# A decoder block on one core: the networks' down products and the mixers' output held by tokens, with the weights as the 512-wide moving operand

## The chip, the core and the metric

The kernel runs on one core of one Trainium2 chip. The metric is the device time of one execution in microseconds. The engines are TensorE (PE, with its weight loads PEld), VectorE (DVE), ScalarE (ACT), GpSimd (POOL) and SyncE (SP); each works through its own instructions in order, and they wait for each other by semaphores.

## What is computed

A decoder block on 512 tokens of 1024 features, all in fp32:

```python
h = x
h = h + 0.5 * swiglu(rms_norm(h, g_ffn1), w_gate1, w_up1, w_down1)      # hidden width 2816
z = rms_norm(h, g_mix) @ w_in                                          # conv GLU | q | k | v | gates
y_conv = conformer_conv(a_glu, ...)                                    # depthwise, width 31
y_attn = (dilated window attention, 3 groups of 4 heads) @ w_attn_out
h = h + (sigmoid(gA) * y_conv + sigmoid(gB) * y_attn) @ w_mix_out
h = h + 0.5 * swiglu(rms_norm(h, g_ffn2), w_gate2, w_up2, w_down2)
h = h + sigmoid(rms_norm(h, g_ple) @ w_ple_gate) * (p @ w_ple_proj)
y = rms_norm(h, g_final)

def swiglu(x, w_gate, w_up, w_down):
    return (silu(x @ w_gate) * (x @ w_up)) @ w_down
def rms_norm(x, g):
    return x * rsqrt(mean(x * x, -1) + EPS) * g
```

## The kernel before

A product of two fp32 matrices is made of three matmuls on rounded operands: each operand is split into a high and a low part (`xsh`, `xsl`; `wh`, `wl`; `bh`, `bl`), and high x high, high x low and low x high are summed in PSUM (`mm3`, L458 to L460). A split is a copy by ACT that rounds and a subtraction by DVE. For most weights the low part is made by a copy of the negated high part and a DMA from POOL's queue that adds the raw weights (L374, L376).

The activations are held by features: a tile of 128 features by 512 tokens. The weights are the stationary operand and the tokens move. The tokens stand in four classes of 128 (token modulo four), since the attention needs them so; `by_class` reads a tile in that order, with a stride of four elements, and `classes` writes or reads one that is already in it. In before the order is made at the first network's last adds (L723) and in the first convolution products.

Each network's gate and up products run over eleven pairs of 128 hidden features. Two pairs (`EARLY = 2`) are plain products, 512 wide; the nine others are done in quarters, seven products in place of eight (`quarters_of`, L712, L713, L715), each 256 columns wide, with sums of weight quarters (L342 to L355) and of operand halves (`normed`, L806 for x; `form_pair`, L643, by POOL for the hidden values). The plain pairs need only the scaled x, since the norm's factor per token, R, is multiplied into their results (L774, L777). R comes from `Norm`: ACT squares (L567), DVE adds the squares (L575), PE sums them over the features (`ss`, L586), DVE finds the root by tokens (`by_token`, L589 to L594), writes it on diagonals (L598), and PE spreads it over all partitions (`on_all`, L603, L604). Then `normed` makes x times gain times R (`xn`, L811) and forms the nine pairs' operands from it.

Down products are made in three rounds of three pairs (`ROUNDS`), each for two groups of four feature tiles, in quarters, 256 tokens wide; then one plain round (`down_plain`). `add` (L727, L730) adds them to the residual `h`, times one half. The same quarters make the mixers' output (`mx`). At the end of a network, `into` splits the new residual for the next step, tile by tile. The last step, the gate of the per-layer embedding, works by tokens, and turns `h` there with transposes (`turned`, L1615).

The order of the work is the order in which the code issues it: `PLAN` lists the steps of a network, `slab` fetches, sums and splits weights some steps ahead, and jobs put aside (`job`) are issued by `work(t)` for as long as they fit into t us of ACT and DVE, or one by one after products (`QUOTA`, `AFTER`). `N_NORM` says in which plain pair, half and k the norm's two steps are issued. `background` issues the rotary tables' rows (`TABLES`, `TABLES_D`).

## Time and profile before

| | us |
|---|---|
| median of 3 runs | 1283.06 (1282.82 to 1283.29) |
| the profiled execution's span | 1280.8 |
| first network | about 0 to 354 |
| projections, convolution, attention, gates | about 354 to 829 |
| mixers' output | about 829 to 870 |
| second network | about 870 to 1210 |
| embedding gate and last norm | about 1210 to 1281 |

The span runs from the first to the last instruction of one profiled execution. Rows of a timeline give start, busy time, engine, line of the code, operation and tile, shape and count, and in brackets how long the engine was idle ahead of it and what ended that. Rows of the groups give count, busy time in all and mean ns of one, then the idle time ahead of them. Rows of the windows give from and to, the length, and for PE, PEld, DVE, ACT and POOL the busy time and the count of instructions, then the granted clock, the busy share of the DMA engines and GB/s. PE's matmuls overlap, so that their rows are longer than the distance between them.

### The profile page before, as it was taken

To read this page: it belongs to the slowest core of one execution; us is meant where nothing else is said; L and a number is where in the kernel's file an instruction comes from. 1 tells how busy PE (TensorE), PEld (TensorE's weight loads), DVE (VectorE), ACT (ScalarE), POOL (GpSimd) and SP (SyncE) were. 2 spreads that over 40 slices of the span, in tenths; PEclk is the share of its full clock that TensorE was granted. 3 is DMA by queue.
4 is the path that set the end of the run, shared out by engine and by line. 5 is a ranking of instruction groups with operands and counts; after the bars stand their busy time and mean duration, and the time that the engine had idled before them with its cause. 6 is when DMAs were issued, how large, how long until landed. Compare 5 with 4: busy or idle time off the path is not lost.

```text
span 1280.8 us, 21791 instructions
## 1 busy us (share of the span) xinstructions
PE 1267.4 (99%) x8266; PEld 1163.6 (91%) x8266; DVE 1015.3 (79%) x1617; ACT 740.9 (58%) x1088; POOL 299.8 (23%) x392
## 2 busy tenths in 40 slices
PE   9999999999999999999999999999999999999997
PEld 7899999998988888989898888898899999998986
DVE  6988778898969887878778755786988888786875
ACT  6677566575643264746565445373677566585662
POOL 3122222132223232333232222012122122132000
PEclk9999999999999999999999999999999999999999
DMA  9676876867879889898887788657576876867641
GB/s 302 148 171 161 204 201 157 206 165 191 193 177 227 213 152 204 155 188 150 173 183 166 168 190 218 160 119 211 132 177 159 203 206 146 208 168 187 155 115 50
DMA packets 114128, 226.12 MB, mean 177 GB/s; under 512 B 20584, under 2 KB 50664, under 8 KB 114024
## 3 DMA queue, kind: packets, MB, share of 16 engines
q0 software_dynamic: 49600, 142.10, 54.6%
q1 hardware_dynamic: 64136, 82.37, 20.1%
q8 instruction: 65, 1.06, 0.3%
q14 instruction: 39, 0.32, 0.1%
q10 hardware_dynamic: 288, 0.26, 0.1%
HBM read 168.56 MB, written 2.13 MB: 133 GB/s over the span
## 4 chain that ended last, share of the span: by engine, by line
PE 76%; DVE 2%; issue 0%; ACT 0%; DVEq 0%
PE pa L712 5%; PE pa L713 5%; PE pa L715 5%; PE pq L458 4%; PE pq L459 4%; PE pq L460 4%; PE pg L458 3%; PE pg L460 3%; PE pg L459 3%; PE pd L713 3%; PE pd L715 3%; PE pd L712 3%; PE pb L459 2%; PE pb L460 2%; PE pb L458 2%; PE pe L713 1%
## 5 line engine op out<-in xcount | busy, mean ns | idle before, releaser
L376 POOL DMA_DIRECT2D wl<-wr x108 | 93.4, 867 | 440.4 <-ACT wl L374 341.1
L712 PE MATMUL pa<-bh,wh 128*128 128x256 f32 x680 | 167.6, 284 | 0.5 <-DVE gx L727 0.4
L713 PE MATMUL pa<-bl,wh 128*128 128x256 f32 x680 | 167.3, 283 | 0.0
L1098 DVE SCALAR_TENSOR_TENSOR acc<-glu,taps,acc 128x511 f32<-128x511 f32 (+14 forms) x240 | 161.6, 732 | 0.0
L405 DVE TENSOR_TENSOR wl<-s,wh 128x1024 fp32r<-128x1024 f32 (+1 forms) x96 | 108.5, 1132 | 38.0 <-ACT wh L404 37.8
L374 ACT ACTIVATE wl<-wh 128x1024 fp32r<-128x1024 f32 x84 | 87.9, 1051 | 81.9 <-DMA wh<-in_w_in 50.8
L712 PEld LDWEIGHTS pa<-bh,wh 128*128 128x128 f32 x680 | 130.6, 192 | 1.0 <-issue 0.5
L713 PEld LDWEIGHTS pa<-bl,wh 128*128 128x128 f32 x680 | 130.8, 192 | 0.0
L374 ACT ACTIVATE wl<-wr 128x1024 fp32r<-128x1024 f32 (+1 forms) x108 | 105.7, 979 | 24.3 <-DVE wl L405 11.4
L404 ACT ACTIVATE wh<-s 128x1024 fp32r<-128x1024 f32 (+1 forms) x96 | 93.0, 969 | 38.8 <-PE pd L459 14.7
L388 ACT ACTIVATE wh<-wr 128x1024 fp32r<-128x1024 f32 (+1 forms) x108 | 105.5, 977 | 11.0 <-PE pd L715 6.1
L712 PE MATMUL pd<-bh,wh 128*128 128x256 f32 x448 | 110.3, 284 | 0.0
L713 PE MATMUL pd<-bl,wh 128*128 128x256 f32 x448 | 110.2, 283 | 0.0
L376 POOL DMA_DIRECT2D wl<-in_w_in x56 | 48.5, 869 | 219.6 <-ACT wl L374 200.5
L715 PE MATMUL pa<-bh,wl 128*128 128x256 f32 x680 | 97.0, 283 | 0.0
L458 PE MATMUL pq<-xsh,wh 128*128 128x512 f32 x224 | 88.8, 396 | 0.0
L715 PEld LDWEIGHTS pa<-bh,wl 128*128 128x128 f32 x680 | 88.4, 192 | 0.0
L459 PE MATMUL pq<-xsl,wh 128*128 128x512 f32 x224 | 87.4, 390 | 0.0
L460 PE MATMUL pq<-xsh,wl 128*128 128x512 f32 x224 | 87.4, 390 | 0.0
L713 PEld LDWEIGHTS pd<-bl,wh 128*128 128x128 f32 x448 | 86.2, 192 | 0.0
L712 PEld LDWEIGHTS pd<-bh,wh 128*128 128x128 f32 x448 | 86.1, 192 | 0.1
L458 PE MATMUL pg<-xsh,wh 128*128 128x512 f32 x192 | 76.1, 396 | 0.2 <-ACT xsh L478 0.2
(330 smaller groups left out, 3616.0 us busy)
## 6 DMA issues: line engine op xcount, KB each, us to landing
wl<-wr POOLq DMA_DIRECT2D x72, 512.0 KB, 5.7
wh<-in_w_in POOLq DMA_DIRECT2D x56, 512.0 KB, 7.0
wl<-in_w_in POOLq DMA_DIRECT2D x56, 512.0 KB, 6.0
wr<-in_w_ffn_up SPq DMA_DIRECT2D x80, 256.0 KB, 4.4
wr<-in_w_ffn_gate SPq DMA_DIRECT2D x78, 256.0 KB, 4.8
wr<-in_w_ffn_down SPq DMA_DIRECT2D x96, 192.0 KB, 3.8
wl<-wr POOLq DMA_DIRECT2D x36, 384.0 KB, 4.4
wr<-in_w_ffn_down SPq DMA_DIRECT2D x16, 256.0 KB, 4.1
```

The lines of the kernel that those rows point to most:

```text
L374: A.activation(l.bitcast(F32R), h, AF.Copy, scale=-1.0)
L376: G.dma_start(to, src, accum_op=OP.add)
L388: A.activation(h, r, AF.Copy)
L404: A.activation(h, r, AF.Copy)
L405: V.tensor_sub(l, r, h.bitcast(F32))
L458: PE.matmul(ps, wh, xh, start=start, stop=False, skip_group_check=part)
L459: PE.matmul(ps, wh, xl, start=False, stop=False, skip_group_check=part)
L460: PE.matmul(ps, wl, xh, start=False, stop=stop, skip_group_check=part)
L712: PE.matmul(o, h[:, c], th, start=q in ("B11", "B21", "T1") and i == 0, stop=False, skip_group_check=True)
L713: PE.matmul(o, h[:, c], tl, start=False, stop=False, skip_group_check=True)
L715: PE.matmul(o, l[:, c], th, start=False, stop=i >= len(at) - 2, skip_group_check=True)
L1098: bg.append(lambda acc=acc, g=g, w=w, s=s: V.scalar_tensor_tensor(acc[:, s:], g[:, :S - s], w, acc[:, s:], op0=OP.mult, op1=OP.add))
```

## The change

The residual `h` is now held by tokens: four blocks of 128 tokens by 1024 features. In the down products and the mixers' output the hidden values (or the mixed ones) are the stationary operand, and the weights move, 512 wide, read in four pieces of 128 (`rows_of`, L738 to L743). A round of down products takes two pairs and makes all features, so that there are five rounds; `EARLY` is 1, and ten gate and up pairs are done in quarters. The adds work on 512 features of a token block, with the factor per token `half_r` (0.5 r, L863), in which up's R is held.

```diff
-EARLY = 2
-ROUNDS = ((0, 2), (2, 3), (5, 3), (8, 3))
+EARLY = 1
+ROUNDS = ((0, 1), (1, 2), (3, 2), (5, 2), (7, 2), (9, 2))
-N_NORM = {"1": ((0, 1, 2), (0, 1, 7)), "2": ((0, 0, 6), (0, 1, 3))}
+N_NORM = {"1": ((1, 2), (1, 7)), "2": ((0, 6), (1, 3))}
+    def rows_of(ps, q, h_, l_, xs_, beside=None):
+        h_, l_ = (z.rearrange("p (m k i) -> p k m i", m=4, k=len(xs_)) for z in (h_, l_))
+        at = [(ps[g], slice(g * P, (g + 1) * P), k, *x_) for k, x_ in enumerate(xs_) for g in range(2)]
+        for o, c, k, th, tl in at:
+            PE.matmul(o, th[:, c], h_[:, k], start=q in ("B11", "B21", "T1") and k == 0, stop=False, skip_group_check=True)
+            PE.matmul(o, tl[:, c], h_[:, k], start=False, stop=False, skip_group_check=True)
+        if beside:
+            beside()
+        for o, c, k, th, tl in at:
+            PE.matmul(o, th[:, c], l_[:, k], start=False, stop=k == len(xs_) - 1, skip_group_check=True)
+    def add(q, ps, factor=None):
+        x_, half = GOES[q]
+        for i, p in enumerate(ps):
+            b = 2 * half + i
+            t = h[b][:, x_ * S:(x_ + 1) * S]
+            if factor is None:
+                V.tensor_add(t, t, p)
+            else:
+                V.scalar_tensor_tensor(t, p, factor[:, b:b + 1], t, op0=OP.mult, op1=OP.add)
```

The pairs' operands are formed from the scaled x without R: three of the quarters' operands are the plain pair's own splits, the sums come from `u`, a copy of the scaled x (in the first network by ACT at L1070, in the second beside each new split at L1086). R is multiplied into the gate's results (L918). The forming is issued between the two halves of the plain pair:

```diff
+            for c in range(4):
+                for q, (k, half) in {"B11": (c, lo), "B21": (c + 4, lo), "B22": (c + 4, hi)}.items():
+                    xn[c][q] = tuple(z[:, half] for z in xs[k])
+            u = made()
+        done = []
+        for half in range(2):
+            us_ = [slab(("gq", n, 0, 2 * half + i)) for i in range(2)]
+            fs = {k: f for (at, k), f in zip(N_NORM[n], (token, lambda: R.append(norm.on_all()))) if at == half}
+            if soon_ and half == 0:
+                fs[2] = soon_
+            done.append(plain(us_, fs))
+            if half == 0:
+                forms()
                 work(10.9)
-        xs.clear()
-        done = R = None
+        gated(*done)
+        work(10.9)
@@ gate_up
+                    if q != "T3":
+                        zs = z.rearrange("p (c s) -> p c s", s=256)
+                        r_ = both_halves(lo if q == "B21" else hi)
+                        job(lambda zs=zs, r_=r_: V.tensor_mul(zs, zs, r_), 0, 0.69)
@@ begin
-            xs.append(split(x[c], "xs", gain(V_G1, c)))
+            xs.append(split(by_class(x[c]), "xs", gain(V_G1, c), by=classes))
```

The classes' order is thus made at the very start, by strided reads. Where the layouts meet there are transposes by PE: of x into `h` during the first gate and up pair (`row_block`, L1077, 32, with strided stationary operands), and of `h` into the next step's operands at three places (`flipped`, L764, 96, four feature tiles between the two passes of the last product T4, four after the next step's k = 1). The 32 of the last step are gone. Where the norms are of `h`, the squares are summed by ACT while it squares (`Rows`, L624), without PE's `ss`. The pairs' subtractions are issued on DVE:

```diff
-    def form_pair(x1, x2, parts_, tile_=None, first_of=None, by=FORMS):
+    def form_pair(x1, x2, parts_, tile_=None, first_of=None, by=V):
+    class Rows(Norm):
+        def add(self, b, x_):
+            A.activation(T("sq"), h[b][:, x_ * S:(x_ + 1) * S], AF.Square, scale=D ** -0.5,
+                         accum_out=self.cols[:, x_ * NB + b:x_ * NB + b + 1])
+    def flipped(k, v, n):
+        p = bank("tp")
+        for b in range(NB):
+            PE.transpose(p[:, b * P:(b + 1) * P], h[b][:, k * P:(k + 1) * P], ident)
+        return p, split(p, n, gain(v, k))
```

How this moves instructions shows at three places. The first is DVE early in the first network, before, from the last sums of squares (L575) to the first rows of the norm by tokens (L589 and on; L423 is a weight's split):

```order
L575 TENSOR_TENSOR sq_150<-sq_150,sq_194 128x512
L575 TENSOR_TENSOR sq_150<-sq_150,sq_197 128x512
L423 TENSOR_TENSOR wl_208<-wr_121,wh_207 128x1024
L589 TENSOR_SCALAR m_307<-ss_302 128x4
L552 TENSOR_SCALAR t_309<-m_307 128x4
```

The same place in the changed kernel, from the last split of plain weights (L422) on; L341 is a sum of weights, L835 half a sum of u, L825 the low part of such a sum:

```order
L422 TENSOR_TENSOR wl_218<-wr_128,wh_217 128x1024
L341 TENSOR_TENSOR s_50_221<-wr_169,wr_172 128x1024
L835 TENSOR_TENSOR t_286<-u_278 128x256
L835 TENSOR_TENSOR t_286<-u_282,t_286 128x256
L835 TENSOR_TENSOR t_287<-u_279 128x256
L835 TENSOR_TENSOR t_287<-u_283,t_287 128x256
L835 TENSOR_TENSOR t_288<-u_280 128x256
L835 TENSOR_TENSOR t_288<-u_284,t_288 128x256
L825 TENSOR_TENSOR bl_291<-t_286,bh_290 128x512
```

and the end of that stretch, up to the norm's rows, of which the first is now L587:

```order
L835 TENSOR_TENSOR t_301<-u_283,u_279 128x256
L835 TENSOR_TENSOR t_301<-u_283,t_287 128x256
L825 TENSOR_TENSOR bl_297<-t_289,bh_296 128x512
L835 TENSOR_TENSOR t_304<-u_284,u_280 128x256
L835 TENSOR_TENSOR t_304<-u_284,t_288 128x256
L345 TENSOR_TENSOR s_87_342<-s_50_221,wr_175 128x1024
L349 TENSOR_TENSOR wr_169<-wr_175,wr_169 128x1024
L587 TENSOR_SCALAR m_364<-ss_367 128x4
L551 TENSOR_SCALAR t_366<-m_364 128x4
```

Between the weight's split and the norm's first row there are now 21 rows: fourteen L835, four L825 and three sums of weights.

The second place is ACT at the same time in the changed kernel: L421 is the plain pair's last weight, L373 and L387 the first quarter's weights, L1070 makes u, L822 the high part of a sum of u:

```order
L421 ACTIVATE wh_217<-wr_128 128x1024
L373 ACTIVATE wl_223<-wr_175 128x1024
L387 ACTIVATE wh_224<-wr_175 128x1024
L1070 ACTIVATE u_278<-gx 128x512
L1070 ACTIVATE u_279<-x_103,gx 128x512
L1070 ACTIVATE u_280<-x_104,gx 128x512
L1070 ACTIVATE u_281<-x_105,gx 128x512
L1070 ACTIVATE u_282<-x_106,gx 128x512
L1070 ACTIVATE u_283<-x_107,gx 128x512
L1070 ACTIVATE u_284<-x_108,gx 128x512
L1070 ACTIVATE u_285<-x_109,gx 128x512
L822 ACTIVATE bh_290<-t_286 128x512
```

The eight rows of u stand behind the two copies of `wr_175`, and the first high part behind all eight; in before none of these rows was there.

The third is the entry of the second network on DVE, changed: L478 are the low splits of the four low and then the high feature tiles, L752 the mixers' last adds, L422 and L341 weights:

```order
L478 SCALAR_TENSOR_TENSOR xsl_8712<-tp_8706,gx,xsh_8711 128x512
L478 SCALAR_TENSOR_TENSOR xsl_8723<-tp_8717,gx,xsh_8722 128x512
L752 TENSOR_TENSOR gx<-gx,pa_8524 128x512
L752 TENSOR_TENSOR gx<-gx,pa_8525 128x512
L422 TENSOR_TENSOR wl_8740<-wr_8600,wh_8739 128x1024
L422 TENSOR_TENSOR wl_8744<-wr_8617,wh_8743 128x1024
L341 TENSOR_TENSOR s_1377_8747<-wr_8642,wr_8645 128x1024
L478 SCALAR_TENSOR_TENSOR xsl_8774<-tp_8768,gx,xsh_8773 128x512
```

and later on ACT there: the last formed parts (L822), the weights of the second quarter product (L373, L387), R (L612), gate's silu (L811) and the weights of the third product, T2 (L403):

```order
L822 ACTIVATE bh_8902<-t_8901 128x512
L373 ACTIVATE wl_8935<-wr_8651 128x1024
L387 ACTIVATE wh_8936<-wr_8651 128x1024
L612 ACTIVATE R_8964<-R_8961 128x512
L822 ACTIVATE bh_8905<-t_8904 128x512
L811 ACTIVATE tg_8996<-tg_8996 128x512
L811 ACTIVATE tg_8997<-tg_8997 128x512
L403 ACTIVATE wh_9016<-s_1432_8933 128x1024
```

The last adds stand behind four low splits on DVE, and T2's weights behind the formed parts and both silus on ACT; in before a second plain pair lay between the forming and the first quarter product.

More of the change, by code (lines that the diff above doesn't have):

```diff
@@ L737, in ffn @@
+    h = [res[:, b * D:(b + 1) * D] for b in range(NB)]
+    def ffn(n, xs, made, norm, out_, soon_=None, last_=None):
         hid = {}
@@ L1585, in block_kernel @@
         for b in range(NB):
+            if j == 0 and b == 2:
+                over(gs, V_GP, high)
+                ending.pop()()
             if j and b == 3:
```

404 lines of the change are left out of this document (180 added, 224 removed).

## The prediction

> **What bounds the kernel now.** I read the page first: span and the busy time by engine, then the slices.
>
> ```profile
> span 1280.8 us, 21791 instructions
> PE 1267.4 (99%) x8266; PEld 1163.6 (91%) x8266; DVE 1015.3 (79%) x1617; ACT 740.9 (58%) x1088; POOL 299.8 (23%) x392
> PE   9999999999999999999999999999999999999997
> PEclk9999999999999999999999999999999999999999
> ```
>
> TensorE (PE) is busy in 99% of the span, at full granted clock in every slice, so the time is the sum of its matmuls plus the few places where it waits. VectorE (DVE) has 265 us left over the whole span, which says nothing of a single stage. So I price the matmuls first and then look for each place where PE, which works in order, would come to an instruction whose operand is not there. The profile shows a matmul's modelled length, not its cost; the cost is the distance from start to start, from the timeline of PE:
>
> ```profile
> 101.13 0.28 PE L712 MATMUL pd<-bh,wh 128*128 128x256 f32 x1
> ...
> 102.94 0.28 PE L713 MATMUL pd<-bl,wh 128*128 128x256 f32 x1
> 12.09 0.40 PE L459 MATMUL pu<-xsl,wh 128*128 128x512 f32 x1
> ...
> 17.99 0.39 PE L458 MATMUL pg<-xsh,wh 128*128 128x512 f32 x1
> 1221.84 0.96 PE L586 MATMUL ss<-mean,sq 128*128 128x1 f32 x8
> 1222.66 0.61 PE L1591 MATMUL pp<-wh,wh 128*128 128x512 f32 x1
> 1223.10 0.40 PE L1592 MATMUL pp<-wh,wl 128*128 128x512 f32 x1
> ...
> 1224.28 0.38 PE L1615 MATMUL hT<-ident,h 128*128 128x128 f32 x2
> ...
> 1224.93 0.38 PE L1615 MATMUL hT<-ident,gx 128*128 128x128 f32 x2
> ```
>
> Fifteen steps of 256 columns take 1.81 us, 120.5 ns each; 26 steps of 512 columns take 5.90 us, 227 ns each. One wide step thus replaces two narrow ones for 14 ns less. Six transposes take 0.65 us, 109 ns each. Four sums of squares by PE (eight records) take 0.82 us. The five `pp` matmuls from 1223.10 to 1224.28 take 236 ns each, though they are 512 wide: their stationary tile is read with a stride, and their weight loads are the slow ones:
>
> ```profile
> L458 PEld LDWEIGHTS pg<-xsh,wh 128*128 128x128 f32 x192 | 36.1, 188 | 7.9 <-ACT xsh L478 0.7 <-PE pg L460 0.2
> L1591 PEld LDWEIGHTS pp<-wh,wh 128*128 128x128 f32 x16 | 5.0, 311 | 0.0
> ```
>
> **What PE itself does, both networks together.** Down products: 1512 matmuls of 256 and 192 of 512 become 840 + 96 of 512: 182.2 + 43.6 - 212.5 = 13.3 us less. Gate and up, with one plain pair less and one pair of seven products more: 384 of 512 and 3024 of 256 become 192 and 3360: 87.2 + 364.4 - 43.6 - 404.9 = 3.1 less. Mixers' output: 336 of 256 become 168 of 512: 2.4 less. Twelve sums of squares go to ScalarE (ACT): 2.5 less. 128 new transposes against 32 old ones: 96 x 0.109 = 10.5 more. Together 10.8 us less.
>
> Two prices are not in the trace. The 32 transposes of L1077 read x at a stride of four: between 109 ns and the 236 of `pp`, 0 to 4.1 us; I take 4.0, since those slow loads are the only strided ones. The 1104 matmuls whose weights now move in four pieces of 128 cost 227 ns, or 236 as `pp`, which moves such pieces too: 0 to 9.9 us; I take 0, since the slow load already explains `pp`. PE's own balance: **-6.8**.
>
> **The wait for R in the first network.** This decides the forecast. In before, the chain that turns sums of squares into R follows the last square on DVE at once, and PE finds R ready:
>
> ```profile
> 20.21 1.22 DVE L423 TENSOR_TENSOR wl<-wr,wh 128x1024 fp32r<-128x1024 f32 x1
> 21.69 0.16 DVE L589 TENSOR_SCALAR m<-ss 128x4 f32<-128x4 f32 x1 [0.26 <-PE ss L586]
> ...
> 25.27 0.96 DVE L598 TENSOR_SCALAR diag<-ident,yl 128x128 fp32r<-128x128 f32 x4
> 28.47 0.39 PE L603 MATMUL R<-diag,one_r 128*128 128x512 f32 x1
> ```
>
> The chain runs 21.69 to 26.23, 4.54 us, and PE comes at 28.47: 2.2 us of cover. After the change PE does the same work up to this point, but on DVE fourteen half-width subtractions (L835), four splits (L825) and three sums of weights stand between the last square and the chain's first row, as the order above shows. Their prices, as distances between starts:
>
> ```profile
> 16.09 1.22 DVE L423 TENSOR_TENSOR wl<-wr,wh 128x1024 fp32r<-128x1024 f32 x1
> 17.22 3.08 DVE L575 TENSOR_TENSOR sq<-sq,sq 128x512 f32<-128x512 f32 x4
> 29.77 0.69 DVE L774 TENSOR_TENSOR tg<-pg,R 128x512 f32<-128x512 f32 x1 [3.54 <-ACT R L610]
> 30.38 0.68 DVE L774 TENSOR_TENSOR tg<-pu,R 128x512 f32<-128x512 f32 x1
> 51.50 0.42 DVE L806 TENSOR_TENSOR t<-xn,xn 128x256 f32<-128x256 f32 x1
> 51.84 0.42 DVE L806 TENSOR_TENSOR t<-xn,t 128x256 f32<-128x256 f32 x1
> 9.73 0.71 ACT L478 ACTIVATE xsh<-gx 128x512 fp32r<-128x512 f32 x1
> 10.35 0.62 ACT L567 ACTIVATE sq<-gx 128x512 f32<-128x512 f32 x1
> 14.89 1.05 ACT L422 ACTIVATE wh<-wr 128x1024 fp32r<-128x1024 f32 x1
> 15.84 1.67 ACT L567 ACTIVATE sq<-gx 128x512 f32<-128x512 f32 x3
> 17.40 1.06 ACT L422 ACTIVATE wh<-wr 128x1024 fp32r<-128x1024 f32 x1
> 20.45 1.06 ACT L374 ACTIVATE wl<-wh 128x1024 fp32r<-128x1024 f32 x1 [1.98 <-DMA wh<-in_w_ffn_gate]
> ```
>
> DVE: 1.13 us for 1024 columns, 0.61 for 512, 0.34 for 256. ACT: 0.62 with a scale, 0.95 for 1024. The subtractions need u, which ACT makes behind two 1024-wide copies that wait for weights. ACT is free at 18.46; these weights came by 20.45 in before; I take 19.0. Then 2 x 0.95 and 8 x 0.62: the last u at 26.0, the first split's high half 0.62 later, and its release 0.2 after that: 26.8. From there DVE still has four splits (2.4), eight subtractions (2.7), two sums (2.3) and the chain (4.54): R's operand is ready at 38.7. PE comes at 28.47 + 1.0 (the next part) + 0.23 for R's first half: **9.0 us of wait**. It is 8.5 to 10.5 with the weights at 18.5 to 20.5, and 1 to 2 more if ACT reads x's stride slowly. Nothing covers it: R stands in PE's queue ahead of the plain pair's last six matmuls, and each engine works in its own order.
>
> The 1.0: x is now split from a strided view. DVE's strided reads here cost 0.62 us for 256 columns
>
> ```profile
> L723 DVE SCALAR_TENSOR_TENSOR h<-pa,gx x4: 617/620/625, 328.0 to 333.1; 128x256 f32<-128x256 f32 x4
> L730 DVE SCALAR_TENSOR_TENSOR h<-pa,h 128x256 f32<-128x256 f32 x32 | 12.1, 419 | 5.4 <-PE pa L715 5.2
> ```
>
> against 0.42, so 0.4 for 512, times eight: 3.2 us, of which DVE's gaps before 12 us swallow two: **+1.0** (0 to 3).
>
> **Second half of the first network.** Here the tables of the rotary embedding run too. DVE is given R's multiplications (20 x 0.61), the pairs' subtractions from GpSimd (POOL) (36 x 0.34) and the adds by token, and loses what POOL cost it:
>
> ```profile
> L658 DVE TENSOR_TENSOR bl<-u,bh 128x512 fp32r<-128x512 f32 x18 | 30.0, 1667 | 0.0
> L658 DVE TENSOR_TENSOR bl<-t,bh 128x512 fp32r<-128x512 f32 x40 | 26.9, 685 | 1.1 <-ACT bh L655 1.1
> 196.00:354.00 158.00, 157.19 (x1192) 150.69 (x1192) 139.25 (x184) 99.51 (x134) 39.86 (x50) 1.00 0.78 184
> 1030.00:1210.00 180.00, 179.64 (x1410) 175.28 (x1409) 140.53 (x175) 119.23 (x159) 42.37 (x52) 1.00 0.75 183
> ```
>
> The same split takes 1667 ns while POOL subtracts and 685 otherwise. The rows from the second down round to the tenth pair, each at its distance, give 155 to 159 us for DVE against PE's 158 in the first window, where it was busy for 139 before: **+1.5** (0 to 6). In the second network there are no tables; a pair costs DVE 16.9 us against PE's 20.2, and that hides.
>
> **Entry of the second network.** With `u` made beside each new operand, ACT needs 1.24 us for one k, and DVE's adds of the last product stand behind the fourth low split. Counted from the first transpose (T): the fourth split ends at T + 5.7, the two adds at T + 6.95; PE has done k = 0 and 1 at T + 5.4 and ends the other transposes at T + 8.6, not 7.15: 1.5. R's chain and the formings then end on DVE at T + 33.5, and ACT's split for T2 stands behind both silus: T + 36.4, where PE wants it at 34.0: 2.4; the low half for B21 is late by about as much. **+4.0** (0 to 7).
>
> **What goes.** PE's waits in the second half of the first network (158.00 - 157.19 = 0.8 in the windows above) and of the second (180.00 - 179.64 = 0.4), where the low halves of the plain pairs' hidden values now come during the pair before, and these two:
>
> ```profile
> L712 PE MATMUL pa<-b,wh 128*128 128x256 f32 x248 | 61.0, 284 | 1.1 <-DVE h L730 1.1
> L1593 PE MATMUL pp<-wl,wh 128*128 128x512 f32 x16 | 6.6, 412 | 0.6 <-DVE wl L423 0.6
> ```
>
> The first is the mixers' start; there DVE's added rows cost 1.5 again, net +0.4. The others: -1.8. What is late next at the network's end is the low transposes, which lie between T4's two passes and hide there.
>
> **Sum:** -6.8 + 9.0 + 1.0 + 1.5 + 4.0 + 0.4 - 1.8 = +7.3 on the profiled 1280.8 us, 1288.1. The median of the runs, 1283.06, lies 2.3 above that execution's span: **1290.4 us**.
>
> **The rivals.** (a) *The wait for R is short*, the one that ends on the other side. Place: PE's R, DVE's rows ahead of it. Price: each us by which the operand comes before 38.7 is one us less; without wait 1281.4, and below 1.7 us of wait the kernel is not slower than before. For it: DVE has gaps ahead of the splits. Against: the last u alone, at 26.0, leaves 12 us of DVE work. (b) *The later covers hold*: transposes at 109 ns, entry and second half hidden: 1290.4 - 4.0 - 4.0 - 1.5 = 1280.9. For it: DVE's mean load of 79%; against: the queues just counted. (c) *Wide weights in pieces cost `pp`'s 236 ns*: +9.9, 1300.3. (d) *DVE bounds the second half*: 6 instead of 1.5, and 7 at the entry: 1297.9. (e) *The clock falls in the wait*: no gap of PE in before is over 0.3 us after its start, so no row shows what 9 us do; if the next 4.2 us ran at half speed (as long as the warming matmuls that fill 1.06 to 5.25), it would lose 2.1: 1292.5.
>
> The Trainium skill, "TensorE: Matmul & The Clock Gate", section "What's actually happening", bears on (e): after an idle window of about 3.4 us the array falls to half rate until it has been busy for as long. By that rule the loss is an estimated 1.7 us and the time 1292.1. The slices' PEclk never leaves 9, so no run here shows it yet. On POOL's subtractions, "SBUF — State Buffer", section "Who interferes with whom", says that a DVE instruction with two SBUF inputs contends with GpSimd reads. The 1667 against 685 ns agree; had DVE kept those prices, moving the work would be worth the more.
>
> **How the numbers follow.** Forecast 0.50, (a) 0.07, (b) 0.15, (c) 0.08, (d) 0.10, (e) 0.10. Slower by over 0.2% (2.6 us, about what a measurement of this kernel can tell from no change) means over 1285.6: the forecast but for a margin, (c), (d), (e): 0.74. (a) and (b) lie at the lower border of no change: 0.15 same, 0.11 faster. The range runs from a little under (a) and (b), 1279, past (c), to 1302.
>
> **What would show it.** PE idle before L605 for 8 to 10 us near 30 us, ended by DVE's diag; u's last row at 26; L587's first row on DVE near 34; PE gaps of 1.5 to 3 us in the second network's first 40 us; L1077's loads near 311 ns; moving weights at 227 ns. A gap at L605 under 4 us, or wide matmuls at 236 ns, would make the prediction wrong.

## The result and the profile after

| | before | after |
|---|---|---|
| median of 4 runs, us | 1282.94 (1282.71 to 1283.29) | 1316.78 (1315.06 to 1317.51) |
| the profiled execution's span, us | 1280.8 | 1313.3 |

The changed kernel takes 1.026 times as long (95% interval 1.0247 to 1.0274), 33.8 us more; forecast were 7.3 more. The sign was right, the size was not, and the time lies above the range. The page of the changed kernel begins:

```profile
span 1313.3 us, 20051 instructions
...
PE 1270.6 (97%) x7546; PEld 1127.2 (86%) x7546; DVE 1067.7 (81%) x1717; ACT 772.4 (59%) x1114; POOL 219.5 (17%) x284
...
PE   8599999999999999999999999998999999999997
...
PEclk9799999999999999999999999999999999999999
```

The second slice of PE has fallen to 5, and in it, for the first time, the granted clock to 7. To see all of PE's waits I took, from its timeline, the distance between the starts of neighbouring matmuls, less the usual distance for that shape (227, 120 and 109 ns), and summed what is left by stage. The rest of the span is PE's own work.

| us | before | after | difference | forecast |
|---|---|---|---|---|
| PE's own work (span less all waits) | 1265.9 | 1256.7 | -9.2 | -6.8 |
| waits from the start to R | 3.9 | 23.6 | +19.7 | +10.0 |
| R to 160 us before the first network's end | 0.1 | 2.7 | +2.6 | 0 |
| last 160 us of the first network | 1.8 | 10.4 | +8.6 | +0.7 |
| projections to gates | 4.7 | 4.8 | +0.1 | 0 |
| mixers' output | 1.4 | 1.0 | -0.4 | +0.4 |
| first 50 us of the second network | 0.1 | 11.8 | +11.7 | +4.0 |
| rest of the second network | 0.8 | 2.2 | +1.4 | -0.4 |
| embedding gate, last norm | 2.0 | 0.2 | -1.8 | -0.6 |

The rows add to the span's difference of 32.5 within rounding. PE did gain what was promised, and three stages lost 40 us. A wait can bring the granted clock down, and what the slower products behind it cost is then counted in the same row (see the clock below).

**The start.** ACT's timeline of the changed kernel, and DVE's and PE's behind it:

```profile
6.00 1.23 ACT L477 ACTIVATE xsh<-x,gx 128x512 fp32r<-128x512 f32 x1
...
14.47 1.12 ACT L566 ACTIVATE sq<-x 128x512 f32<-128x512 f32 x1
...
27.75 1.22 ACT L1070 ACTIVATE u<-gx 128x512 f32<-128x512 f32 x1
28.87 7.77 ACT L1070 ACTIVATE u<-x,gx 128x512 f32<-128x512 f32 x7
...
44.69 0.15 DVE L587 TENSOR_SCALAR m<-ss 128x4 f32<-128x4 f32 x1
...
33.96 0.39 PE L459 MATMUL pu<-xsh,wl 128*128 128x512 f32 x1
48.35 0.77 PE L605 MATMUL R<-diag,one_r 128*128 128x512 f32 x1 [14.00 <-DVE diag L600]
49.04 0.80 PE L606 MATMUL R<-diag,one_r 128*128 128x512 f32 x1
...
51.91 0.28 PE L728 MATMUL pa<-xsh,wh 128*128 128x256 f32 x1
```

The mechanism is the forecast one: PE stands idle at L605, DVE's diag ends the wait, and the norm's first row stands behind the forming. But the last u ends at 36.6, not at 26.0, and L587 starts at 44.69, not near 34. Every ACT row that reads x by class takes 1.1 to 1.2 us; before, the same shapes took 0.71 (the split) and 0.62 (the square). DVE's split of the strided x takes 1142 ns, 0.4 more than before's 0.75, which is the price the forecast used.

**The clock.** Windows of the changed kernel, from and to, then PE, PEld, DVE, ACT, POOL and the granted clock:

```profile
40.00:50.00 10.00, 1.65 (x3) 1.12 (x4) 9.55 (x34) 3.27 (x5) 0.86 (x1) 0.50 0.47 105
...
51.00:52.00 1.00, 1.00 (x5) 0.82 (x4) 0.97 (x2) 0.51 (x1) 0.00 (x0) 0.72 0.00 0
52.00:53.00 1.00, 1.00 (x11) 1.00 (x10) 1.00 (x3) 0.00 (x0) 0.00 (x0) 1.00 0.11 29
10.00:20.00 10.00, 8.02 (x25) 5.41 (x24) 7.08 (x10) 10.00 (x11) 0.00 (x0) 0.83 1.04 371
20.00:37.00 17.00, 13.80 (x61) 10.61 (x61) 10.23 (x16) 17.00 (x17) 1.00 (x1) 1.00 0.27 71
...
296.10:316.10 20.00, 17.56 (x79) 14.20 (x80) 17.83 (x24) 10.94 (x14) 2.29 (x3) 0.91 0.75 184
```

After 14 us without work PE begins at half clock and is back at full clock about 3 us later. Rival (e) did happen. The row from 20 us shows ACT ahead of the wait: it works for 17.00 of 17.00 us.

The 0.83 and the 0.91 are two more such falls, to 0.50 from 14.0 to 17.4 us and from 307.6 to 311.0. No long idleness stands ahead of them: PE was busy for 1.86 of the 3.42 us before the one and for 1.77 of the 3.41 us before the other. Nor does such a stretch always do it: in the run with the tables sooner (below) the same wait of 1.44 us at 307 left the clock at 1.00. The first of the two cost next to nothing, as PE would have waited for its operands anyway (it comes to R at 34.2 us, and at 34.07 in the run with the norm first, where the clock was 1.00). The second cost 1.6: eight products took 3.43 us in place of 1.82.

**The second network's entry.** ACT, DVE and PE of the changed kernel:

```profile
898.47 0.69 ACT L1086 ACTIVATE u<-tp,gx 128x512 f32<-128x512 f32 x1 [0.82 <-DVE xsl L478]
899.05 0.68 ACT L477 ACTIVATE xsh<-tp,gx 128x512 fp32r<-128x512 f32 x1
900.55 0.69 ACT L1086 ACTIVATE u<-tp,gx 128x512 f32<-128x512 f32 x1 [0.82 <-DVE xsl L478]
...
899.77 0.75 DVE L478 SCALAR_TENSOR_TENSOR xsl<-tp,gx,xsh 128x512 fp32r<-128x512 f32 x1 [1.33 <-ACT xsh L477]
...
901.29 0.50 PE L457 MATMUL pu<-xsh,wh 128*128 128x512 f32 x1 [1.12 <-ACT u L1086]
...
905.42 0.30 PE L764 MATMUL tp<-ident,gx 128*128 128x128 f32 x1 [1.79 <-ACT u L1086]
```

ACT's copy u waits 0.82 us for DVE's low split, though it uses nothing of it; both read one PSUM tile. Split, low split and u so run one behind the other, 2.08 us for each k, where the forecast had 1.24 and PE needs 1.36 (six matmuls of 227 ns). PE waits at each k, and then 2.2 us more for the low weights of B21.

**The last 160 us of the first network.** What PE itself waited for there (in all, times, longest), and ACT's and DVE's timeline ahead of the longest wait, at 307:

```profile
PE pa L738 <- DVE gx L754: 1.4, 1, 1.4
PE pa L728 <- ACT p L900: 1.4, 2, 0.7
PE pa L728 <- DVE p L913: 1.4, 2, 0.8
PE pe L743 <- DMA wl<-wr: 1.3, 2, 1.1
PE pd L968 <- DMA wl<-wr: 0.9, 1, 0.9
```

```profile
302.76 0.68 DVE L905 TENSOR_TENSOR u<-pa,p 128x512 f32<-128x512 f32 x1
305.40 1.23 DVE L404 TENSOR_TENSOR wl<-s,wh 128x1024 fp32r<-128x1024 f32 x1 [1.95 <-ACT wh L403]
306.55 1.40 DVE L754 SCALAR_TENSOR_TENSOR gx<-pa,half,gx 128x512 f32<-128x512 f32 x2
...
303.81 0.61 ACT L671 ACTIVATE bh<-u 128x512 fp32r<-128x512 f32 x1
304.33 1.99 ACT L403 ACTIVATE wh<-s 128x1024 fp32r<-128x1024 f32 x2
```

No engine is full here: in the 20 us around it (the last row of the clock's windows) DVE works for 17.83 us and ACT for 10.94. DVE's sum u (L905) releases ACT's high part, behind which a weight's high part stands; DVE stands 1.95 us waiting for that, and the adds that PE wants stand behind the weight's low part. At this wait a late row of DVE is so paid twice. The 10.4 us of the stage hold 1.6 of the clock's fall behind it.

**What held.** Wide products, transposes of the strided x, the embedding's products and a split by DVE, in the changed kernel:

```profile
1000.97 0.39 PE L738 MATMUL pa<-wh,bh 128*128 128x512 f32 x1
...
1002.78 1.07 PE L743 MATMUL pa<-wl,bh 128*128 128x512 f32 x4
...
54.79 0.65 PE L1077 MATMUL tp<-ident,x 128*128 128x128 f32 x4
```

```profile
L1627 PE MATMUL pp<-wl,wh 128*128 128x512 f32 x16 | 6.4, 397 | 0.0
L674 DVE TENSOR_TENSOR bl<-t,bh 128x512 fp32r<-128x512 f32 x44 | 29.6, 683 | 1.1 <-ACT bh L671 1.1
```

Eight wide steps take 1.81 us, 226 ns each, as taken. Four transposes start 122 ns apart ((0.65 - 0.283) / 3, 283 ns being the record of one), not 236: 0.4 us for all 32 over the usual distance, and not 4.0. Their weight loads take 210 ns (141 for the transposes of `h`), not 311. `pp`'s wait has gone.

### The profile page after: what moved, and what is told of

Read it like the earlier page. It is cut to its first block, busy times and chain, and to the rows that moved or that the text cites. A ratio compares the mean times of both kernels' runs of the same rounds, so it can differ in the third digit from the quotient of the medians.

```text
span 1313.3 us, 20051 instructions
## 1 busy us (share of the span) xinstructions
PE 1270.6 (97%) x7546; PEld 1127.2 (86%) x7546; DVE 1067.7 (81%) x1717; ACT 772.4 (59%) x1114; POOL 219.5 (17%) x284
## 4 chain that ended last, share of the span: by engine, by line
PE 81%; DVE 8%; ACT 4%; DMA 4%; issue 2%; DVEq 0%; POOL 0%; SPq 0%; ACTq 0%; POOLq 0%
PE pa L728 5%; PE pa L731 5%; PE pa L729 5%; PE pq L457 4%; PE pq L458 4%; PE pq L459 4%; PE pa L738 3%; PE pa L739 3%; DMA wl<-wr 3%; PE pa L743 2%; PE pg L457 2%; PE pg L459 2%; PE pg L458 2%; PE pd L729 2%; PE pd L728 2%
## 5 line engine op out<-in xcount | busy, mean ns | idle before, releaser
L404 DVE TENSOR_TENSOR wl<-s,wh 128x1024 fp32r<-128x1024 f32 x96 | 117.1, 1220 | 54.2 <-ACT wh L403 54.1
L728 PE MATMUL pa<-bh,wh 128*128 128x256 f32 x480 | 118.6, 285 | 2.8 <-ACT p L900 1.4
L403 ACT ACTIVATE wh<-s 128x1024 fp32r<-128x1024 f32 x96 | 100.5, 1050 | 33.2 <-PE pd L739 10.5
L729 PE MATMUL pa<-bl,wh 128*128 128x256 f32 x480 | 117.7, 283 | 0.0
L373 ACT ACTIVATE wl<-wr 128x1024 fp32r<-128x1024 f32 x104 | 108.9, 1047 | 11.2 <-PE pd L743 5.0
L373 ACT ACTIVATE wl<-wh 128x1024 fp32r<-128x1024 f32 x76 | 79.5, 1050 | 54.4 <-DMA wh<-in_w_in 38.3
L387 ACT ACTIVATE wh<-wr 128x1024 fp32r<-128x1024 f32 x104 | 108.8, 1046 | 3.9 <-PE pd L743 3.2
L458 PE MATMUL pg<-xsl,wh 128*128 128x512 f32 x160 | 64.1, 401 | 2.9 <-DVE xsl L478 2.7
L459 PE MATMUL pg<-xsh,wl 128*128 128x512 f32 x160 | 63.3, 396 | 0.0
L754 DVE SCALAR_TENSOR_TENSOR gx<-pa,half,gx 128x512 f32<-128x512 f32 x80 | 56.1, 743 | 2.6 <-PE pa L743 2.6
L738 PE MATMUL pa<-wh,bh 128*128 128x512 f32 x136 | 54.3, 400 | 1.5 <-DVE gx L754 1.4
```

Of the source, the lines that this page charges most:

```text
L373: A.activation(l.bitcast(F32R), h, AF.Copy, scale=-1.0)
L387: A.activation(h, r, AF.Copy)
L403: A.activation(h, r, AF.Copy)
L404: V.tensor_sub(l, r, h.bitcast(F32))
L458: PE.matmul(ps, wh, xl, start=False, stop=False, skip_group_check=part)
L459: PE.matmul(ps, wl, xh, start=False, stop=stop, skip_group_check=part)
```

## The experiments

Each time is that of one run, with one of before beside it (1283.06 to 1283.83 us). "Waits" are those of the table above. The changed kernel's own four runs lie 2.4 us apart, and the profiled one, with which the spans are compared, is the fastest of them, so that a span that differs by 2 or 3 us shows little alone. A fall of the clock costs about 1.6 us for each 3.4 us of PE's work at 0.50, and it comes behind different waits in different runs.

### The start: what makes R late

**No stride.** x is read as it lies; every queue keeps its order.

```diff
-xs.append(split(by_class(x[c]), "xs", gain(V_G1, c), by=classes))
+xs.append(split(x[c], "xs", gain(V_G1, c)))
-norm.add(by_class(x[c]), classes)
+norm.add(x[c])
-A.activation(classes(t), by_class(x[k]), AF.Copy, scale=gain(V_G1, k))
+A.activation(t, x[k], AF.Copy, scale=gain(V_G1, k))
```

> The changed kernel with x read as it lies: its split, its squares and the making of u read x without a stride, so the tokens of the first network are not put into classes, which leaves out a part of what is computed. Everything else, the order of every queue included, is the changed kernel's. Theory (ACT's strided reads made R late: 24 rows at about 0.5 us each): the first scaled x at 0.72 and u and the squares at 0.62 us per row, the last u near 26 to 28 instead of 36.6, PE's wait ahead of R 9 to 10 us instead of 14.2, the excess up to R 14 to 16 instead of 23.6, and the span 1304 to 1307. Rival (the wait is made by DVE's rows or by the weights, which stay): the wait stays over 13 and the span over 1310.

1307.95 us, span 1306.2. Groups of the first 45 us, and PE's wait:

```profile
L478 DVE SCALAR_TENSOR_TENSOR xsl<-x,gx,xsh 128x512 fp32r<-128x512 f32 x7 | 5.2, 747 | 1.0 <-ACT xsh L477 1.0
...
L1070 ACT ACTIVATE u<-x,gx 128x512 f32<-128x512 f32 x7 | 4.4, 707 | 0.0
L566 ACT ACTIVATE sq<-x 128x512 f32<-128x512 f32 x7 | 4.1, 617 | 0.0
```

```profile
39.11 0.77 PE L605 MATMUL R<-diag,one_r 128*128 128x512 f32 x1 [9.32 <-DVE diag L600]
```

PE begins R at 39.1 (forecast: 38.7), waits 9.3 to 9.5 us for it (9.0), and all waits up to R are 14.6, not 23.6. Once ACT reads without a stride, the chain that was forecast holds, each station 1.0 to 1.5 us late: the last u ends at 27.4 (26.0), L587 starts at 35.5 (near 34), the chain ends at 39.75 (38.7). That R is within half a microsecond is partly luck, as PE starts its first half before the chain's end. The stride costs the other 9.0, half of it at R and half ahead of it. The kernel gains 7.1 of these; 1.5 comes back at the second network's entry (13.3), where in this run the clock is at 0.50 twice for 3.4 us, from 898 and from 932; at the changed kernel's entry it is 1.00 throughout.

**A busy wait.** Sixty matmuls that nobody reads fill PE's wait.

```diff
+p = bank("wm", "cv")
+for _ in range(60 if n == "1" else 0):
+    PE.matmul(p, one_r, xs[0][0], start=True, stop=True)
 R.append(norm.on_all())
```

> First network: 60 matmuls of 512 columns, whose result nothing reads, stand in PE's queue ahead of R's, so that PE is busy while it waits for R. Theory (the granted clock falls to 0.5 in the 14 us of idleness and stays there for some 3 us): with PE busy the clock stays 1.00, R's two matmuls and the six after it stand 227 ns apart instead of up to 692, span 1.7 us shorter, 1311 to 1312. Rival (the long distances behind the wait come from the operands, not the clock): they stay, span unchanged or longer.

1311.46 us, span 1309.7. PE of this kernel, and a window:

```profile
48.16 0.50 PE L606 MATMUL R<-diag,one_r 128*128 128x512 f32 x1 [0.23 <-DVE diag L600]
...
49.88 0.28 PE L728 MATMUL pa<-xsh,wh 128*128 128x256 f32 x1
```

```profile
49.00:51.00 2.00, 2.00 (x15) 1.83 (x14) 2.00 (x5) 1.33 (x3) 0.00 (x0) 1.00 0.07 9
```

R still comes late (0.9 us sooner), but the clock stays at 1.00, and from R's second matmul to the first quarter product pass 1.72 us in place of 2.87: the clock's price is 1.15 us, with a little at R's first matmul. Rival (e) had 2.1. The span falls by 3.6; the rest is the sooner R and later stages, such as the last 160 us of the first network with 9.4, where the clock stays at 1.00 too. The Trainium skill, "TensorE: Matmul & The Clock Gate", section "What's actually happening", has half rate after an idle window of about 3.4 us, until the array has been busy as long; 14 us of idleness and some 3 us of half clock agree with it. The two other falls of the changed kernel, with PE busy for over half of the 3.4 us ahead, don't fit an idle window, and there the measurement decides.

**u read once.** One strided copy of x makes u, and the split and the square read without a stride. The first convolution's norm reads its sums in another order of tokens here, which changes what is computed.

```diff
-xs.append(split(by_class(x[c]), "xs", gain(V_G1, c), by=classes))
+A.activation(classes(us0[c]), by_class(x[c]), AF.Copy, scale=gain(V_G1, c))
+xs.append(split(us0[c], "xs"))
```

> First network: x is read with a stride once per tile, by ScalarE for u; the two halves of the split and the forming read u, the squares read x as it lies (PE reads their sums with a stride). 8 strided rows on ScalarE instead of 24, none on VectorE. Theory (a strided read costs ScalarE about 0.55 us more for 512 columns): u's 1.12 us rows stay, squares fall to 0.52 and high parts to 0.52, the eight u rows of 8.9 us ahead of the forming are gone; PE reaches R at about 34, R's operand is ready near 43 instead of 48.3: span 1307 to 1309. Rival (the ScalarE rows were slow because VectorE or the DMAs disturbed them): contiguous rows are slow too, R stays near 48.

1314.26 us, span 1312.5. R comes at 44.8 instead of 48.35, and the waits up to it only fall to 20.1: PE's wait at R is 5.7 instead of 14.0, but the first splits now stand behind the strided copies, and PE reaches R 4.9 us later. Of the 3.5 us won the span keeps 0.8, since between the projections and the gates the waits rise from 4.8 to 8.4 in this run.

### The formed parts: where they stand

**The norm first.** In the first network the norm's rows are issued ahead of the forming.

```diff
+if n == "1" and half:
+    fs[2] = lambda: (token(), forms(), work(10.9))
-if half == 0:
+if half == 0 and n == "2":
```

> First network only: the norm's chain by tokens is issued ahead of the forming of the quarters' operands (both at k = 2 of the plain pair's second half). Theory (R waits because its chain stands behind the forming on VectorE): the 14.2 us wait at R falls below 2 us and the clock does not fall behind it; the forming, now later, makes PE wait about 5 us at the third product (T2) instead; span 1304 to 1309 against 1313.3. Rival (the chain itself or the sums of squares are late, order does not matter): the wait at R stays above 8 us and the span within 3 us.

1307.18 us, span 1305.3. R is in time (34.07), but PE stands at the first pair's third product:

```profile
49.81 0.58 PE L728 MATMUL pa<-bh,wh 128*128 128x256 f32 x1 [6.47 <-ACT p L902]
```

Up to R waits are 9.3, at the first pair 9.4 (1.0 before): of 14.3 us gained 8.4 are given back, with the half clock once more.

**Formed in two parts.** The parts for T1 and T2 first, those for T3 and T4 behind the gate's rows; squares read x without a stride.

```diff
-            for c, t12 in enumerate(t12s):
+            def others():
+                for c, t12 in enumerate(t12s):
...
+            return others
```

> First network: the norm's chain ahead of the forming, as in e1; the forming in two parts, that for T1 and T2 ahead of the gate of the plain pair, that for T3 and T4 behind it; the squares read x as it lies, and PE reads their sums with the stride. Theory: no wait at R; squares 0.52 us instead of 1.1, so PE reaches R 2 to 3 us sooner than in the changed kernel (34.2); the third product waits 2 to 4 us instead of e1's 6.6; span 1296 to 1301. Rival (e1's wait at the third product comes from u, the strided rows, and not from what stands ahead of the gate): the wait there stays at 5 us or more, span above 1302.

1304.88 us, span 1303.1. Up to R 7.3, first pair 9.8: the third product's wait has gone (0.6), and now PE waits 4.9 us at T3 for DVE's low part (L827). So the rival had the span and not the place. A run with this, the second network's edits below and earlier tables together took 1305.93 us (span 1304.2) where 1287 to 1296 was expected; its rival, that the waits are one debt of DVE and ACT that only moves on, had given over 1299.

**A second plain pair.** Before's second plain pair is put back, 20 us of PE without formed parts; norm first, contiguous squares, and the entry's edit below.

```diff
-PLAN = (("gu", 1), ("gu", 2), ("gu", 3), ("dn", 1), ("gu", 4), ("gu", 5), ("dn", 2), ("gu", 6), ("gu", 7), ("dn", 3),
+PLAN = (("gu", 2), ("gu", 3), ("dn", 1), ("gu", 4), ("gu", 5), ("dn", 2), ("gu", 6), ("gu", 7), ("dn", 3),
+        for half in range(2):
+            us_ = [slab(("gq", n, 1, 2 * half + i)) for i in range(2)]
+            done.append(plain(us_, {}))
+            work(10.9)
```

> Each network gets its second plain gate and up pair back (its down products stay in quarters by tokens), with the norm's chain ahead of the forming in the first network, the squares read as x lies, and e4's entry. PE is given 2 x 1.6 us more work. Theory (what the changed kernel lost at the first pair and the entry is cover: forming the quarters' operands takes VectorE and ScalarE some 15 to 20 us, which lay beside the second plain pair before and now stands ahead of the first quarter products): no wait at R, the first quarter pair's waits fall from 9 to 11 us in e1, e6 and e10 to under 2, the entry's from 9 to under 6, span 1288 to 1295. Rival (strided reads and weights are late whatever lies between): 6 us or more stay at the first quarter pair, span above 1300.

1299.12 us, span 1297.3: 16 us less than the changed kernel, though PE itself has 2.3 us more to do (the span less all waits is 1259.0, not 1256.7). The waits are 7.4 up to R, 5.7 behind it, 1.0 at the first quarter pair, 5.0 at the second network's entry. The longest wait behind R, like the longest of the entry (2.3 us), is for R's copy, which on ACT stands behind the forming: behind u and four high parts in the first network, behind the high parts and two weights' copies at the entry. This run changes several things at once, the second plain pair being the one that the runs before it lack:

```profile
38.71 0.74 PE L457 MATMUL pu<-xsh,wh 128*128 128x512 f32 x1 [3.84 <-ACT R L613]
```

**The forming behind R**, in both networks, and then in the first network behind the gate too:

```diff
-zip(N_NORM[n], (token, lambda: R.append(norm.on_all())))
+zip(N_NORM[n], (token, lambda: (R.append(norm.on_all()), forms(), work(10.9))))
```

> The second plain pair of before put back, as in the run before this one, but in both networks the making of u and of the sums is issued behind R, so that nothing stands between the norm and R's copy on ACT and DVE. Theory (the formed parts were a debt that needs a cover of one plain pair, and behind R they have it): the excess at R and the first quarter pair falls from 14.1 (7.4, 5.7, 1.0) to 5 to 7, that of the second network's entry from 5.0 to 2.5 to 4, the span from 1297.3 to 1287 to 1291. Rival (the debt only moves on to the first quarter product): those sums stay within 2 us and the span over 1295.

```diff
 gated(*done)
+if n == "1":
+    forms()
```

> As the run with the formed parts behind R, but in the first network they are issued behind the first plain pair's gate as well (its products with R, silu and up), so that the two PSUM banks of that pair come free before the forming, and the second plain pair's 20 us of PE lie over it. Theory (the formed parts need 12 us of ACT and DVE with nothing of PE's behind them, and this is such a place): the 9.8 us behind R go to under 1.5, no more than 3 us appear at the first quarter pair, the second network's entry stays at 2.0, and the span is 1289 to 1292. Rival (a debt that only moves on): 5 us or more appear at the first quarter pair, and the span stays over 1295.

1301.73 and 1297.32 us, spans 1300.0 and 1295.5. PE's longest wait behind the first network's R, in the one and in the other, with ACT's row that was late in the second:

```profile
52.14 0.80 PE L457 MATMUL pg<-xsh,wh 128*128 128x512 f32 x1 [6.74 <-DVE tg L816]
```

```profile
56.62 0.76 PE L459 MATMUL pg<-xsh,wl 128*128 128x512 f32 x1 [5.31 <-DMA wl<-in_w_ffn_up]
...
49.74 1.04 ACT L373 ACTIVATE wl<-wh 128x1024 fp32r<-128x1024 f32 x1
```

In the second network the theory held: the entry's waits fall to 2.0, of which 1.5 are the last adds ahead of the transposes. In the first it fell twice: the waits behind R are 9.8, for the gate's rows (and with them the PSUM banks), and 7.9, for the second plain pair's low weights, whose first step on ACT stands behind u and the formed parts. Some 2.5 us of each are the half clock behind the wait. It is not the first quarter pair (1.0 in both), so the rivals had the span (over 1295) and not the place. Seven orders were tried in the first network, the changed kernel's among them, and in each the forming, some 9 us of strided u and 5 of high parts on ACT with its sums and low parts on DVE, is late itself or delays what stands behind it in one of the two queues. That no order hides it isn't shown.

### The second network's entry

**u ahead of the low split.** ACT copies u from PSUM behind the high part, and DVE subtracts from u.

```diff
+A.activation(hh, p, AF.Copy, scale=gain(v, k))
+A.activation(us_[k], p, AF.Copy, scale=gain(v, k))
+V.tensor_sub(ll, us_[k], hh.bitcast(F32))
```

> Entry of the second network only: u is copied from PSUM ahead of the low part, and the low part is u minus the high part, so that VectorE does not read that PSUM tile and ScalarE does not wait for it. Theory (u's wait for the low part's read of the same PSUM tile makes 2.08 us per k, where PE needs 1.36): 1.2 to 1.3 us per k, PE's waits between 900 and 920 fall from 7.4 us to under 2.5, span 1306.5 to 1309. Rival (ScalarE's weights or VectorE's last adds bound the entry): waits of 5 us and more stay, span within 2 us of 1313.3.

1312.12 us, span 1310.3. The group of u, and PE's waits from 890 to 945:

```profile
L1094 ACT ACTIVATE u<-tp,gx 128x512 f32<-128x512 f32 x8 | 5.9, 734 | 0.0
```

```profile
PE pe L731 <- DMA wl<-wr: 4.1, 1, 4.1
PE tp L764 <- DVE gx L752: 1.5, 2, 1.3
```

u no longer waits (0.0 in place of 6.6), a k takes 1.15 us, and PE's waits at each k are gone. But PE now comes sooner to B21, whose low weights stand behind the formed parts on ACT: 4.1 in place of 2.2, and behind that wait the clock falls (2.0 us). The entry falls from 11.8 to 8.9, the span by 3.0. Both the theory and the rival were half right: the order on the PSUM tile made the waits at each k, and the weights bound what is left.

**And formed in two parts** there, so that these weights come sooner:

> Second network's entry: as e4, and the forming in two parts as in e6. Theory (after e4 the low part of the second product's weights, issued by ScalarE behind seven formed parts, was what came last): it is issued behind four, about 4 us sooner, and PE's wait there (4.3 us in e4) goes; PE's excess in the entry 11.8 us in the changed kernel, 8.9 in e4, here under 5; span 1304 to 1307. Rival (that transfer is late by the DMA queue itself): 4 us of wait stay, span 1309 or more.

1314.90 us, span 1313.1. B21's wait is gone, and 4.0 us stand at T3 for DVE's last low part: entry 9.5, again with some 2 us of half clock. With this copy of u, the cover of a second plain pair and the forming behind R the entry is 2.0 (above). So the wait on the PSUM tile and the lost cover together account for this stage; no run has the cover alone.

### The last 160 us of the first network

**Tables later**: all of the rotary tables' rows at the network's end.

```diff
-TABLES = {"B21": 1, "T3": 1, "B22": 1, "T1": 1}
-TABLES_D = {"B21": 1, "T3": 1, "B22": 1, "T4": 1}
+TABLES = {}
+TABLES_D = {}
```

> The rotary tables are not issued inside the first network but all at its end (judged by the network's last 160 us, since the tables then stand on VectorE at the start of the projections). PE's distances over the nominal ones in that stretch sum to 10.4 us in the changed kernel and 1.8 before. Theory (VectorE is the bound there: the tables on top of the multiplications by R, the pairs' subtractions and the adds): they fall to 4 us or less. Rival (the waits come from latencies of ScalarE and of the DMAs for the low parts, whatever VectorE's load): 8 us or more stay.

1330.15 us, span 1328.4. PE's waits from 200 to 400:

```profile
PE pb L457 <- ACT xsh L477: 19.5, 1, 19.5
PE pd L968 <- DMA wl<-wr: 0.9, 1, 0.9
```

The stage's waits fall from 10.4 to 2.4, and the clock stays at 1.00 there; the tables' 20 us now stand bare ahead of the projections. The tables are the condition of the 10.4: without them the added rows cost next to nothing (2.4 against 1.8 in before).

**Tables sooner** (from the first down round on, none in the down rounds):

```diff
-if n == "1" and key[1] == 2:
+if n == "1" and key[1] == 1:
-TABLES_D = {"B21": 1, "T3": 1, "B22": 1, "T4": 1}
+TABLES_D = {}
```

> The rotary tables begin one round of down products sooner and are issued in the gate and up products and the plain round alone, so that the same 32 rows spread over more of the network and none stands in a round of down products. Theory (VectorE's load in the last 160 us, where a down round with tables asks more of it than PE takes): PE's excess there falls from 10.4 us to 3 to 6, with nothing new elsewhere; span 1306 to 1311. Rival (any place in this network is as full: the load moves, the wait with it): 9 us or more in the network after its first pair, span within 2 us of 1313.3.

1318.44 us, span 1316.7; the stage has 12.0, with a fall of the clock as in the changed kernel, but at 362, behind a wait of 2.1. The adds at 308 are 1.6 us late as before, though this down round holds no table row: the rows' place in the down rounds is not the cause. Further ahead the waits grow too, from 0.6 to 2.2 between the first pairs and this stage, so that there is no free room there either.

**Other rows of DVE away**: R's multiplications.

```diff
-if q != "T3":
+if q != "T3" and n != "1":
```

> The changed kernel with R's multiplications into the ten quarter pairs left out in the first network, which leaves out the norm's factor there: 20 DVE rows of 0.69 us, one pair's share 1.4 of the 20 us that a pair lasts. Theory (in the second half of the first network DVE's queue is full, so that any row there costs its time): the excess of the last 160 us falls from 10.4 to 2 to 5, the span by 6 to 9, to 1304 to 1307. Rival (the tables cost by what ACT does for them or by where they stand, not by DVE's load): the excess stays above 8 and the span above 1310.

1313.66 us, span 1311.9. The windows that hold the adds at 307, here:

```profile
295.10:315.10 20.00, 18.14 (x93) 14.54 (x91) 17.35 (x23) 12.35 (x15) 3.43 (x4) 1.00 0.74 184
```

Nine rows of 0.69 us are gone from the stage, but its waits fall only from 10.4 to 8.8, and that is no more than the clock: the granted clock is 1.00 here where it was 0.91, and its fall had cost 1.6. The waits for DVE's p (L913) go, 1.4 to 0.2, and others grow by about as much. So it is not load alone. Taking out some 16 us of the tables' rows gave 8.0 us, 6.4 without the clock, 0.4 us of wait for each us of DVE; R's 6.2 us of rows gave about none. The tables' rows are issued right behind the adds of a product, R's as jobs later on; that this place makes the difference is argued, not shown.

**The subtractions back on POOL.**

```diff
-    def form_pair(x1, x2, parts_, tile_=None, first_of=None, by=V):
+    def form_pair(x1, x2, parts_, tile_=None, first_of=None, by=G):
```

> One part undone: the pairs' subtractions go back to GpSimd. Theory (VectorE is the bound in the first network's last 160 us; 18 subtractions of 0.34 us each leave it there, but its other rows slow down beside GpSimd): the excess there falls from 10.4 us to 5 to 8; the start and the entry stay as they are; span 1308 to 1312. Rival (beside GpSimd VectorE loses more than it is spared): 12 us or more, span 1315 or more.

1321.05 us, span 1319.3, 4.3 us slower than the changed kernel's median and 6.0 slower than its profiled run. From 200 to 380:

```profile
L659 POOL TENSOR_TENSOR t<-u,t 128x256 f32<-128x256 f32 x12 | 12.1, 1008 | 0.3
...
L674 DVE TENSOR_TENSOR bl<-u,bh 128x512 fp32r<-128x512 f32 x6 | 5.1, 848 | 0.0
```

A subtraction takes 1008 ns on POOL against 420 on DVE, and DVE's own splits beside it 848 against 684. Moving them to DVE was a gain. And DVE is relieved here, of 23 rows of 0.42 us for some 1.5 us that its splits lose, yet the last 160 us have 11.2 us of waits, none of it the clock's: once more it is not DVE's load alone. The theory's 5 to 8 is false. Another 3.0 us appear in the rest of the second network; their way to PE was not traced.

## Why the prediction was wrong

- **PE's own work, -6.8: -9.2.** Right in the main. The strided transposes cost 0.4 instead of 4.0: the slow loads of `pp` were the wrong row for them. With 0.4 the sum would have been -10.4, and where the other 1.2 us went was not found. Rivals (b), whose waits were to hide, and (c), 236 ns for wide weights, are false.
- **The wait for R, 9.0: 14.2, and the start, 1.0: 5.5 (9.4 less 3.9).** This step failed by its size, and rival (a), a short wait, is false. The chain was right, as the run without a stride shows (39.1 for 38.7, its stations 1.0 to 1.5 us late). But the prediction priced the stride on DVE only, from DVE's rows, and gave ACT "1 to 2 more if ACT reads x's stride slowly". ACT reads x 24 times, at about 0.5 us more each: 12 us on the engine that makes u. ACT was busy without a gap from 20 to 37 us, and DVE's 3.2 us were beside the point. The Trainium skill, "SBUF — State Buffer", section "Specifications (TRN2)", gives 16-byte lines, two hits in a line for the full rate and a penalty for each new line; four fp32 apart, every element is on a new line. ACT's 1.12 against 0.62 us, DVE's 1.14 against 0.75 and PE's loads for the transposes, 210 against 141 ns, agree.
- **The clock, rival (e).** It happened beside the forecast, not instead of it: about 1.2 us where 2.1 were given. Its ground was misread: before does have a gap of over 0.3 us, the 1.1 at the mixers' start that the prediction itself shows (at 836), and behind it the clock stayed at 1.00. A fall behind a shorter wait, for which the sum had no term, cost another 1.6 in the last 160 us.
- **Second half of the first network, 1.5: 8.6 with the waits that were to go.** The step summed DVE's rows against PE's time and so asked only whether DVE is full. It was busy for 146 us of the 160. Of the 8.6, 1.6 are the clock. The tables are the condition of the rest (2.4 without them). What the trace shows at the longest wait, and the step left out, is the exchange of ACT and DVE, in which a late row stops both; that the other waits come the same way isn't shown, and the cause stays open so far. Rival (d) had 6 for it, with DVE's load as its cause; the runs without R's rows and with the subtractions on POOL speak against load alone.
- **Entry of the second network, 4.0: 11.7.** The step took 1.24 us for one k and overlooked the wait of u for the low split, which was in the program; a k took 2.08. What followed, low weights late behind the forming, was named, but not that most of a gain at the transposes would go into it: without a plain pair between, B21's low weights and then T3's low part wait for the forming's end.
- **What goes, -1.8:** `pp`'s part held (-1.8 there alone), the second network's did not (+1.4).

No kernel of these beats before; the nearest, 1297.32, keeps 9.4 us of waits in the first network's second half and 15.7 up to its first quarter pair.

## What to carry to other kernels

When a layout is moved to the place of first use, count the engine that reads it most often, at that engine's own strided price. Where two engines read one PSUM tile, look into the program for the wait between them; the data alone don't show it. Work that is taken out of a stage's front needs a cover: reorder it without one, and the wait moves to what stands behind it. Before a difference of 1 to 2 us between two runs is read as the edit's, see whether the granted clock fell in one of them.

## Not expected of the hardware

ACT's reads of SBUF at a stride of four fp32 took 1.12 us for 128 x 512 against 0.62; PE's transposes from the same tiles started 122 ns apart against 109. PE's loads for them took 210 ns against 141. After 14 us of idleness PE ran at a granted clock of 0.50 for about 3 us, which cost about 1.2 us; it also fell to 0.50 for 3.4 us behind stretches of 3.4 us in which PE was busy for 1.77 and 1.86 us.
